# A merge pass of seven products on one Trainium2 core: the third and fourth product change places, one set of weights is loaded once instead of twice, and one sum moves to VectorE

## The chip, the cores and the metric

The kernel runs on one core of one Trainium2 chip. The metric is device time in microseconds (us) of one execution; the median of three runs is given. A profile of one further execution on the chip goes with it: a record of each instruction on TensorE (PE, with its weight loads as PEld), VectorE (DVE), ScalarE (ACT), GpSimd (POOL), and of each transfer issued by SyncE (SP).

## The reference

One step of a decoder layer, all in fp32: D = 1024, 2048 prompt tokens and 64 sample tokens, so 2112 in all. Two branches (sliding-window attention and gated linear attention) give `o_att` and `o_gla`; the tail below is where the change lies. `r_att` and `r_gla` are columns of the input projection of x.

```
z = einsum('btd,dn->btn', x, w_in)          # q, k, v, ..., r_att, r_gla
o_att, o_gla = attention branch, GLA branch
h      = o_att @ w_pa                       # K = 512
merged = sigmoid(r_att) * h + sigmoid(r_gla) * (o_gla @ w_pg)
y      = layer_norm(alpha * x + merged @ w_o)
```

The kernel's merge stage computes four products of the size (1024 x K) by (K x 2112): `w_pa` (K = 512), and `w_ra`, `w_rg`, `w_pg` (K = 1024 each).

## The kernel before

Products are in fp32 by two halves: an operand is split into a rounded part (`hi`, an ACT cast, L115) and the rest (`lo`, a DVE subtraction, L116), and each product is three matmuls, hi·hi, hi·lo and lo·hi (L1232 to L1234 in the merge stage). PE therefore waits for `wh`, `wl` of the weights and `xh`, `xl` of the tokens.

**The merge stage** lies from 1061.7 to 1644 us of the span. It goes through four passes, objects of the class `Pass`, one for each of the four weights, in the order `w_pa`, `w_ra`, `w_rg`, `w_pg`. Within a pass the matrix product is done as seven half-size products (Strassen's scheme in Winograd's form): weights and tokens are cut in two by two blocks, some products take sums of blocks, and the outputs are sums of products. `ORDER` sets the order of the seven. A product runs over MS = 3 token slices; such a (pass, product, slice) is a unit, and there are 4 x 7 x 3 = 84 of them, n = 0 to 83. A unit has NP4 = 4 column groups of 12 matmuls (6 in `w_pa`), each into one PSUM tile `pa` (five buffers) of 128 x 352.

**Weights.** `raw_w` loads a product's blocks into tiles `ws` (128 x 512 fp32, 256 KB; half of that in `w_pa`), four groups p = 0 to 3 each; `prep_w` forms the sums on POOL in place and splits into `wh`, `wl` (eight buffers each). Product 7 uses w11 − w21, product 6 uses s2 = w21 + w22 − w11, product 5 uses s1 = w21 + w22 and product 3 uses w12 − s2. Loads and splits for a product stand one product (three units) ahead of its use.

**Tokens.** `raw_x` loads `xs` (704 KB, three buffers; `xc` in `w_pa`), `prep_x` splits it into `xh`, `xl` (two buffers each), one unit ahead. The sums of token blocks that products 4 to 7 need are kept in DRAM (`ac_d`, `xc_d`, `uc_d`). Those for the fourth pass, `uc_d`, are formed within the third: at the start of each third unit, n = 42, 45, ... 57, `combine_load` loads two tiles `xc` (L857), `combine_do` forms four sums on POOL (L863 to L866) and stores them on SP (L868).

**Results.** `combine` adds `pa` into tiles `a12` and `a21` (12 buffers each) or a final `fin`. With product 1 in `a12`, product 7 is copied by ACT (L1078) into `a21`; product 6 is added to `a12` by DVE (L1081), and POOL then adds that to `a21` (L1082). The sinks at the end of each output store to `ha_d`, `tt_d` or `mg_d`; in the fourth pass `merge_sink` takes partners `cs` (L1064, four buffers, loaded on SP), a DVE operation (L1110), a POOL addition (L1111) and a store (L1113). The output projection and the normalization follow the merge stage.

Each engine, SP's issuing of transfers included, works its instructions in one fixed order, which a scheduler sets when the program is built, and which is not the order of the code. In it, the `wh` of a product can stand ahead of the `xh` of an earlier unit.

Of the kernel before, what the change touches and what calls it, by code (L numbers as in the profile page):

```python
# [16 lines left out]
ALU = mybir.AluOpType  # L17
# [4 lines left out]
P = 128  # L22
# [10 lines left out]
KT = D // P  # L33
# [18 lines left out]
def kernel(ctx, tc, io):  # L52
    nc = tc.nc
# [12 lines left out]
    def pd():  # L66
        return psd.tile([P, 512], F32, tag="pd", name="pd")

    def pa():
        return psa.tile([P, 512], F32, tag="pa", name="pa")  # L70
# [43 lines left out]
    def split(dst_h, dst_l, src, eng=nc.vector):  # L114
        pin["a"] = nc.scalar.copy(dst_h, src)  # L115
        i = eng.tensor_tensor(dst_l, src, dst_h.bitcast(F32), ALU.subtract)  # L116
        if eng is nc.vector:
            pin["d"] = i
# [3 lines left out]
    pin = {}  # L122
# [430 lines left out]
    for c, (t0, T) in enumerate(CHUNKS):  # L553
# [5 lines left out]
        A = {"kprev": kprev, "vprev": vprev, "q": [], "sil": []}  # L559
# [76 lines left out]
        ps = pd()  # L636
# [215 lines left out]
    def combine_load(new):  # L852
        src, dst, kh, k, s = combos.popleft()
        ts = slice(2 * s * MT, 2 * (s + 1) * MT)
        x1, x2 = new("x1")[:, :2 * MT], new("x2")[:, :2 * MT]
        for x_, k_ in ((x1, k), (x2, kh + k)):
            nc.sync.dma_start(x_, ug_d[k_ // 2][:, k_ % 2, ts] if src is None else src[:, k_, ts])  # L857
        return x1, x2, dst[:, :, s, k]

    def combine_do(x1, x2, dst, eng):  # L860

        t0, t1 = slice(0, MT), slice(MT, 2 * MT)
        eng.tensor_tensor(x2[:, t1], x2[:, t1], x1[:, t1], ALU.subtract)  # L863
        eng.tensor_tensor(x1[:, t1], x1[:, t1], x1[:, t0], ALU.subtract)
        eng.tensor_tensor(x1[:, t0], x1[:, t0], x2[:, t1], ALU.add)
        eng.tensor_tensor(x2[:, t0], x1[:, t0], x2[:, t0], ALU.subtract)  # L866
        for n_, x_ in ((0, x1), (2, x2)):
            nc.sync.dma_start(dst[n_:n_ + 2].rearrange("n p t -> p n t"), x_.rearrange("p (n t) -> p n t", n=2))  # L868
# [23 lines left out]
    for h in range(GH):  # L892
        W2 = {}
        wcap(16 + 6 * h)
        for c, (t0, T) in enumerate(CHUNKS):
# [15 lines left out]
            def combine():  # L911
                if sums:
                    with tc.issue_after(pin["d"].ins):
                        combine_do(*sums.pop(0), nc.vector)

            wv = [wt2("v", 0), wt2("v", 1)]
            for i in range((T + P - 1) // P):
                n = min(P, T - i * P)
                ps = pd()
# [20 lines left out]
            ps = pd()  # L940
            proj(ps[:, :T], wt2("k"), x, T)
            gla_k(B, ps[:, :T])
            combine()
            if len(CHUNKS) - 4 < c < len(CHUNKS) - 1:
                wload()
# [5 lines left out]
            ps = pd()  # L951
            proj(ps[:, :T], wt2("q"), x, T)
            gla_q(B, ps[:, :T])
            tick()
            combine()
            if end:
                chain(B)
            for m in range(2):
# [5 lines left out]
                ps = pd()  # L964
# [23 lines left out]
    ma = right.enter_context(tc.tile_pool(name="ma", bufs=1, side="right", reuse_waits="tile"))  # L988
    T = MT
    NP4 = 4  # L990
    ORDER = (1, 2, 7, 6, 5, 3, 4)
    FINAL = {2: (0, 0), 5: (1, 1), 3: (0, 1), 4: (1, 0)}

    def mtile(tag, n, bufs, dt=F32):
        pool = ma if tag in ("a12", "fin", "xc", "ws", "top") else mb
        return pool.tile([P, n], dt, tag=tag, name=tag, bufs=bufs)

    def toks(s, t):
        return slice((2 * s + t) * T, (2 * s + t + 1) * T)

    class Pass:
# [6 lines left out]

        def raw_w(self, i, p):
            out = []  # L1010
            for c, k in {1: [(1, 1)], 2: [(1, 2)], 7: [(1, 1), (2, 1)], 6: [(2, 1), (2, 2), (1, 1)], 5: [],
                         3: [(1, 2)], 4: [(2, 2)]}[i]:
                t = mtile("ws", KT // 2 * P, 11)[:, :self.kh * P]
                nc.sync.dma_start(t, self.w[c - 1, k - 1, p])
                out.append(t)
            return out

        def prep_w(self, i, p, r):
            A, tt = self.A, nc.gpsimd.tensor_tensor
            if i == 7:  # L1020
                tt(r[0], r[0], r[1], ALU.subtract)
            elif i == 6:
                tt(r[0], r[0], r[1], ALU.add)
                tt(r[2], r[0], r[2], ALU.subtract)
                A[p, "s1"], A[p, "s2"] = r[0], r[2]
            elif i == 3:
                tt(r[0], r[0], A.pop((p, "s2")), ALU.subtract)
            a = A[p, "s2"] if i == 6 else A.pop((p, "s1")) if i == 5 else r[0]
            hi, lo = (mtile(n, KT // 2 * P, 8, F32R)[:, :self.kh * P] for n in ("wh", "wl"))
            split(hi, lo, a)  # L1030
            return hi, lo
# [35 lines left out]
        def combine(self, i, p, s, ps, parts):  # L1067
            acc, z = self.acc, None
            add = nc.vector.tensor_tensor
            if i == 1:  # L1070
                a = acc[p, s, 12] = mtile("a12", T, 12)
                nc.scalar.copy(a, ps)
            elif i == 2:
                z = mtile("fin", T, 6)
                add(z, acc[p, s, 12], ps, ALU.add)
            elif i == 7:
                u = acc[p, s, 21] = mtile("a21", T, 12)
                nc.scalar.copy(u, ps)  # L1078
            elif i == 6:
                a, u = acc[p, s, 12], acc[p, s, 21]  # L1080
                add(a, a, ps, ALU.add)  # L1081
                pin["p"] = nc.gpsimd.tensor_tensor(u, u, a, ALU.add)  # L1082
            elif i == 5:
                a, z = acc[p, s, 12], mtile("fin", T, 6)
                add(z, acc[p, s, 21], ps, ALU.add)
                add(a, a, ps, ALU.add)
            elif i == 3:
                z = acc.pop((p, s, 12))
                add(z, z, ps, ALU.add)
            else:  # L1090
                z = acc.pop((p, s, 21))
                add(z, z, ps, ALU.subtract)
            if z is not None:
                c, t = FINAL[i]
                self.sink(z, parts, 2 * p + c, toks(s, t))
# [13 lines left out]
    def merge_sink(z, parts, ct, ts):  # L1109
# [8 lines left out]
              Pass(io["w_pg"], 4, None, uc_d, [tt_d], merge_sink)]  # L1118
    units = [(q, i, s) for q in passes for i in ORDER for s in range(MS)]
    groups = [(q, i, s, p) for q, i, s in units for p in range(NP4)]  # L1120

    plan = {n: [] for n in range(-2, len(units))}
    for n in range(0, len(units), MS):
        q, i, _ = units[n]
# [65 lines left out]

    for tag, n, bufs in (("a12", T, 12), ("fin", T, 6), ("xc", 2 * T, 5), ("ws", KT // 2 * P, 11), ("top", 640, 1),
                         ("xs", 4 * T, 3),
                         ("a21", T, 12), ("cs", 2 * T, 4), ("xh", KT // 2 * T, 2), ("xl", KT // 2 * T, 2),
                         ("wh", KT // 2 * P, 8), ("wl", KT // 2 * P, 8)):
        mtile(tag, n, bufs, F32R if tag[1] in "hl" else F32)
# [8 lines left out]
    for n, (q, i, s) in enumerate(units):  # L1206
        if n >= 2 * len(ORDER) * MS and n % 3 == 0 and combos:
            with tc.issue_after(pin["x"].ins), tc.issue_after(pin["p"].ins):
                combine_do(*combine_load(lambda t: mtile("xc", 2 * T, 5)), nc.gpsimd)
        if n >= 3 * len(ORDER) * MS and n % 4 == 0 and len(wo) < 4:  # L1210
            with tc.issue_after(pin["x"].ins), tc.issue_after(pin["a"].ins):
# [11 lines left out]
        for p in range(NP4):  # L1223
# [5 lines left out]
            ps = pa()[:, :T]  # L1229
# [209 lines left out]
```

## Time and profile before

| | |
|---|---|
| median of three runs | 1845.85 us (1841.35 to 1847.47) |
| the profiled execution's own time | 1846.22 us |
| its span | 1844.4 us |
| mean granted clock of PE | 0.992 of full speed |
| PE busy in the span | 98% |
| DVE, ACT, POOL busy | 69%, 46%, 23% |
| moved over the span | 315.84 MB, 171 GB/s |

All times below count from the start of the span. In the profile's rows an instruction is given with its line, engine, operation and tiles (out<-in), and behind it, in brackets, the idle time of its engine just before it and what ended that. SPq and ACTq rows are transfers issued by those engines, with the time that issuing took. In a row of stretches the columns are length, busy time of PE, PEld, DVE, ACT and POOL (each with the count of instructions), then the granted clock, the share of time in which the core's DMA engines were busy, and GB/s.

### The profile page before, as it was taken

What the parts mean: (1) busy time and instruction counts of PE and PEld (TensorE: products, weight loads), DVE (VectorE), ACT (ScalarE), POOL (GpSimd) and SP (SyncE); (2) the same over time, 40 slices, a digit from 0 to 9 for tenths busy, and PEclk for the clock granted to TensorE, in tenths of its full rate; (3) what the DMA queues carried; (4) which work ended last, traced back from release to release, by engine and by line L of the source; (5) the groups of instructions that cost most, each with busy time, mean ns of one, the idle gap of its engine ahead of it and who ended that gap; (6) DMA issues with size and microseconds to landing.
All of it is one profiled execution on the core that took longest, in us unless ns stands there. A gap on an engine that the chain in (4) does not pass through costs nothing.

```text
span 1844.4 us, 32399 instructions
## 1 busy us (share of the span) xinstructions
PE 1807.9 (98%) x11683; PEld 1722.2 (93%) x11683; DVE 1280.9 (69%) x2662; ACT 849.9 (46%) x1947; POOL 422.3 (23%) x559
## 2 busy tenths in 40 slices
PE   8999999999999999999999999999999999989997
PEld 7998988899999999999999999999999999988886
DVE  5677778767776776777667669648657566966655
ACT  5444545645665565656546453435443543211110
POOL 3310111300110111011110243430355153631111
PEclk9999999999999999999999999999999999999998
DMA  7211013534345444543543189858887967895531
GB/s 233 63 56 38 12 47 100 165 131 156 120 148 170 143 143 144 186 132 107 181 145 119 58 274 315 283 178 292 276 311 256 310 216 245 287 312 177 166 111 41
DMA packets 199554, 315.84 MB, mean 171 GB/s; under 512 B 21453, under 2 KB 161189, under 8 KB 199376
## 3 DMA queue, kind: packets, MB, share of 16 engines
q1 hardware_dynamic: 192624, 304.61, 50.5%
q0 software_dynamic: 5616, 7.58, 1.5%
q8 instruction: 92, 1.51, 0.3%
q10 hardware_dynamic: 1152, 1.57, 0.3%
q14 instruction: 70, 0.57, 0.1%
HBM read 228.52 MB, written 86.14 MB: 171 GB/s over the span
## 4 chain that ended last, share of the span: by engine, by line
PE 91%; DVE 3%; DMA 3%; issue 1%; POOL 1%; SPq 0%; ACT 0%; DVEq 0%; ACTq 0%; POOLq 0%
PE pd L185 11%; PE pd L187 11%; PE pd L186 11%; PE pa L1234 9%; PE pa L1233 9%; PE pa L1232 9%; PE pd L199 7%; PE pd L198 7%; PE pd L200 7%; PE pa L421 2%; DMA cs<-tt_d 1%; PE pa L406 1%; PE pa L755 1%; PE pa L753 1%; PE pa L754 1%
## 5 line engine op out<-in xcount | busy, mean ns | idle before, releaser
L185 PE MATMUL pd<-x,wh 128*128 128x384 f32 (+2 forms) x1248 | 409.1, 328 | 7.0 <-ACT x L115 6.3
L186 PE MATMUL pd<-x,wh 128*128 128x384 f32 (+2 forms) x1248 | 403.5, 323 | 0.6 <-DVE x L116 0.3
L187 PE MATMUL pd<-x,wl 128*128 128x384 f32 (+2 forms) x1248 | 403.1, 323 | 0.6 <-DVE wl L116 0.6
L1233 PE MATMUL pa<-xl,wh 128*128 128x352 f32 x1176 | 381.3, 324 | 7.9 <-DVE xl L116 7.6
L1232 PE MATMUL pa<-xh,wh 128*128 128x352 f32 x1176 | 381.4, 324 | 2.6 <-ACT xh L115 2.3
L1234 PE MATMUL pa<-xh,wl 128*128 128x352 f32 x1176 | 381.9, 325 | 0.0
L185 PEld LDWEIGHTS pd<-x,wh 128*128 128x128 f32 x1248 | 236.5, 190 | 17.2 <-issue 8.9
L186 PEld LDWEIGHTS pd<-x,wh 128*128 128x128 f32 x1248 | 236.5, 190 | 2.0 <-DVE x L116 1.5
L187 PEld LDWEIGHTS pd<-x,wl 128*128 128x128 f32 x1248 | 236.1, 189 | 1.0 <-DVE wl L116 1.0
L1233 PEld LDWEIGHTS pa<-xl,wh 128*128 128x128 f32 x1176 | 222.7, 189 | 10.4 <-DVE xl L116 10.1
L1232 PEld LDWEIGHTS pa<-xh,wh 128*128 128x128 f32 x1176 | 222.5, 189 | 3.6 <-ACT xh L115 2.6
L1234 PEld LDWEIGHTS pa<-xh,wl 128*128 128x128 f32 x1176 | 224.5, 191 | 0.0
L116 DVE TENSOR_TENSOR xl<-xs,xh 128x1408 fp32r<-128x1408 f32 x63 | 110.5, 1753 | 69.4 <-ACT xh L115 35.7
L198 PE MATMUL pd<-wh,x 128*128 128x256 f32 x512 | 147.9, 289 | 0.0
L199 PE MATMUL pd<-wh,x 128*128 128x256 f32 x512 | 145.6, 284 | 1.2 <-DVE x L116 1.1
L200 PE MATMUL pd<-wl,x 128*128 128x256 f32 x512 | 144.6, 282 | 0.0
L115 ACT CAST x<-xst 128x384 fp32r<-128x384 f32 (+2 forms) x164 | 78.2, 485 | 139.9 <-PE pd L199 117.9
L115 ACT CAST xh<-xs 128x1408 fp32r<-128x1408 f32 x63 | 86.5, 1372 | 103.9 <-PE pa L1234 81.7
L746 POOL TENSOR_SCALAR sq<-sq 128x1 f32<-128x1 f32 (+1 forms) x68 | 21.4, 314 | 467.2 <-ACT ring L745 467.2
L199 PE MATMUL pd<-woh,x 128*128 128x512 f32 x256 | 101.5, 396 | 0.0
L198 PE MATMUL pd<-woh,x 128*128 128x512 f32 x256 | 101.5, 396 | 0.0
L200 PE MATMUL pd<-wol,x 128*128 128x512 f32 x256 | 101.5, 396 | 0.0
(318 smaller groups left out, 3683.6 us busy)
## 6 DMA issues: line engine op xcount, KB each, us to landing
wst<-wt SPq DMA_DIRECT2D x33, 512.0 KB, 3.6
xs<-xc_d SPq DMA_DIRECT2D x24, 704.0 KB, 5.6
cs<-tt_d SPq DMA_DIRECT2D x48, 352.0 KB, 4.7
u<-xT SPq DMA_DIRECT2D x84, 192.0 KB, 4.0
xst<-xT SPq DMA_DIRECT2D x76, 192.0 KB, 2.6
xs<-xT SPq DMA_DIRECT2D x18, 704.0 KB, 5.9
ws<-w_ra SPq DMA_DIRECT2D x36, 256.0 KB, 4.4
ws<-w_rg SPq DMA_DIRECT2D x36, 256.0 KB, 5.6
```

The source lines that it names most:

```text
L115: pin["a"] = nc.scalar.copy(dst_h, src)
L116: i = eng.tensor_tensor(dst_l, src, dst_h.bitcast(F32), ALU.subtract)
L185: mm(ps, hi[:, s], xh[:, :T], start=(k == 0), stop=False)
L186: mm(ps, hi[:, s], xl[:, :T], start=False, stop=False)
L187: mm(ps, lo[:, s], xh[:, :T], start=False, stop=(k == n - 1))
L198: mm(ps, xh[:, xs], hi, start=(k == 0), stop=False)
L199: mm(ps, xl[:, xs], hi, start=False, stop=False)
L200: mm(ps, xh[:, xs], lo, start=False, stop=(k == KT - 1))
L421: mm(ot[pr, :], vb[:, pr], A["pT", bi, kv][:, hf], start=(hf == h0), stop=(hf == 1))
L1232: mm(ps, wh[:, ks], xh[:, ts], start=(k == 0), stop=False)
L1233: mm(ps, wh[:, ks], xl[:, ts], start=False, stop=False)
L1234: mm(ps, wl[:, ks], xh[:, ts], start=False, stop=(k == q.kh - 1))
```

## The change

Product 6 comes ahead of product 7. Product 6 loads three blocks for each group and forms three sums on POOL (lines L1023 to L1025 of the changed kernel): s1 = w22 + w21, s3 = w11 − w21, s2 = s1 − w11, each in place of a block. Product 7 then uses the kept s3 and loads nothing (before, it loaded two blocks and subtracted them); product 5 uses the kept s1 and product 3 the kept s2, as before. A pass has 28 loads of weights instead of 36. When product 7 is done, DVE adds `a12` (which has products 1 and 6 by then) and the PSUM tile into `a21` (L1082 of the changed kernel), in place of ACT's copy of product 7 and POOL's addition. `ws` has 12 buffers in place of 11, and the space comes from the filler `top`.

```diff
-    ORDER = (1, 2, 7, 6, 5, 3, 4)
+    WS, TOP = 12, 128
+    ORDER = (1, 2, 6, 7, 5, 3, 4)
...
-            for c, k in {1: [(1, 1)], 2: [(1, 2)], 7: [(1, 1), (2, 1)], 6: [(2, 1), (2, 2), (1, 1)], 5: [],
+            for c, k in {1: [(1, 1)], 2: [(1, 2)], 6: [(2, 2), (1, 1), (2, 1)], 7: [], 5: [],
                          3: [(1, 2)], 4: [(2, 2)]}[i]:
-                t = mtile("ws", KT // 2 * P, 11)[:, :self.kh * P]
+                t = mtile("ws", KT // 2 * P, WS)[:, :self.kh * P]
...
-            if i == 7:
-                tt(r[0], r[0], r[1], ALU.subtract)
-            elif i == 6:
-                tt(r[0], r[0], r[1], ALU.add)
-                tt(r[2], r[0], r[2], ALU.subtract)
-                A[p, "s1"], A[p, "s2"] = r[0], r[2]
+            if i == 6:
+
+                tt(r[0], r[0], r[2], ALU.add)
+                tt(r[2], r[1], r[2], ALU.subtract)
+                tt(r[1], r[0], r[1], ALU.subtract)
+                A[p, "s1"], A[p, "s2"], A[p, "s3"] = r
             elif i == 3:
                 tt(r[0], r[0], A.pop((p, "s2")), ALU.subtract)
-            a = A[p, "s2"] if i == 6 else A.pop((p, "s1")) if i == 5 else r[0]
+            a = A[p, "s2"] if i == 6 else A.pop((p, "s1" if i == 5 else "s3")) if i in (5, 7) else r[0]
...
+            elif i == 6:
+                a = acc[p, s, 12]
+                add(a, a, ps, ALU.add)
             elif i == 7:
                 u = acc[p, s, 21] = mtile("a21", T, 12)
-                nc.scalar.copy(u, ps)
-            elif i == 6:
-                a, u = acc[p, s, 12], acc[p, s, 21]
-                add(a, a, ps, ALU.add)
-                pin["p"] = nc.gpsimd.tensor_tensor(u, u, a, ALU.add)
+                pin["p"] = add(u, acc[p, s, 12], ps, ALU.add)
```

Most lines of the merge stage have in the changed kernel a number higher by one than before (L1014 has become L1015, L1027 L1028).

Over the program SP has 32 transfers fewer, ACT 48 instructions fewer, POOL 48 fewer and DVE 48 more; the order on PE is the same row by row. The order on the other engines moves. Three places follow; tiles carry their program's own numbers.

**POOL, third pass, units 43 to 46.** Here stand the sums for the third product's weights and the sums for `uc_d` of n = 42 and 45. Before, each of product 7's groups is one L1021:

```order
L1021 TENSOR_TENSOR ws_16722<-ws_16722,ws_16724 128x512
L863 TENSOR_TENSOR xc_16559<-xc_16559,xc_16558 128x352
L864 TENSOR_TENSOR xc_16558<-xc_16558 128x352
L865 TENSOR_TENSOR xc_16558<-xc_16558,xc_16559 128x352
L866 TENSOR_TENSOR xc_16559<-xc_16558,xc_16559 128x352
L1021 TENSOR_TENSOR ws_16806<-ws_16806,ws_16808 128x512
L863 TENSOR_TENSOR xc_16795<-xc_16795,xc_16794 128x352
L864 TENSOR_TENSOR xc_16794<-xc_16794 128x352
L865 TENSOR_TENSOR xc_16794<-xc_16794,xc_16795 128x352
L866 TENSOR_TENSOR xc_16795<-xc_16794,xc_16795 128x352
L1021 TENSOR_TENSOR ws_16894<-ws_16894,ws_16896 128x512
```

Now, on POOL as well, the sums of n = 45 and behind them product 6's groups p = 2 and p = 3:

```order
L863 TENSOR_TENSOR xc_16743<-xc_16743,xc_16742 128x352
L864 TENSOR_TENSOR xc_16742<-xc_16742 128x352
L865 TENSOR_TENSOR xc_16742<-xc_16742,xc_16743 128x352
L866 TENSOR_TENSOR xc_16743<-xc_16742,xc_16743 128x352
L1023 TENSOR_TENSOR ws_16754<-ws_16754,ws_16758 128x512
L1024 TENSOR_TENSOR ws_16758<-ws_16756,ws_16758 128x512
L1025 TENSOR_TENSOR ws_16756<-ws_16754,ws_16756 128x512
L1023 TENSOR_TENSOR ws_16848<-ws_16848,ws_16852 128x512
L1024 TENSOR_TENSOR ws_16852<-ws_16850,ws_16852 128x512
L1025 TENSOR_TENSOR ws_16850<-ws_16848,ws_16850 128x512
```

Behind the sums of n = 45 there stood one weight operation of the third product; now there are six, two groups of three.

**SP, the same place.** Before: the loads for the sums of n = 45, the last of product 7's blocks (ws_16894, ws_16896), and the first blocks of product 6:

```order
L857 DMA xc_16795<-ug3_d_75 128x704
L1014 DMA ws_16894<-w_rg 128x512
L1014 DMA ws_16896<-w_rg 128x512
L1014 DMA ws_16977<-w_rg 128x512
L1014 DMA ws_16979<-w_rg 128x512
L868 DMA uc_d_82<-xc_16794 128x2x352
L868 DMA uc_d_82<-xc_16795 128x2x352
L1045 DMA xs_16804<-xT 128x4x352
L1014 DMA ws_16981<-w_rg 128x512
```

Now, on SP, ws_16754 to 16758 are the blocks of product 6's group p = 2, and ws_16848 to 16852 those of p = 3:

```order
L857 DMA xc_16743<-ug3_d_75 128x704
L1015 DMA ws_16756<-w_rg 128x512
L1015 DMA ws_16758<-w_rg 128x512
L1015 DMA ws_16848<-w_rg 128x512
L1015 DMA ws_16850<-w_rg 128x512
L868 DMA uc_d_82<-xc_16742 128x2x352
L868 DMA uc_d_82<-xc_16743 128x2x352
L1046 DMA xs_16752<-xT 128x4x352
L1015 DMA ws_16852<-w_rg 128x512
```

All blocks of the third product stood ahead of the two stores of n = 45; now one of them, ws_16852, stands behind the stores and an `xs` load.

On ACT and DVE the casts and subtractions of these four weight groups stand in both kernels between the tokens of unit 45 and those of unit 46: `xh` of unit 45, four times a `wh` and a copy of product 1 (L1072, now L1073), `xh` of unit 46. The last two `wh` read ws_16806 and ws_16894 before, and read now ws_16756 and ws_16850, the outputs of L1025.

**POOL, fourth pass, from the third product on.** Before:

```order
L1023 TENSOR_TENSOR ws_18916<-ws_18916,ws_18918 128x512
L1024 TENSOR_TENSOR ws_18920<-ws_18916,ws_18920 128x512
L1027 TENSOR_TENSOR ws_19216<-ws_19216,ws_18739 128x512
L1027 TENSOR_TENSOR ws_19218<-ws_19218,ws_18745 128x512
L1111 TENSOR_TENSOR fin_18567<-fin_18567,cs_18480 128x352
L1027 TENSOR_TENSOR ws_19296<-ws_19296,ws_18836 128x512
L1111 TENSOR_TENSOR fin_18587<-fin_18587,cs_18497 128x352
```

Now:

```order
L1024 TENSOR_TENSOR ws_18564<-ws_18562,ws_18564 128x512
L1025 TENSOR_TENSOR ws_18562<-ws_18560,ws_18562 128x512
L1111 TENSOR_TENSOR fin_18493<-fin_18493,cs_18400 128x352
L1111 TENSOR_TENSOR fin_18513<-fin_18513,cs_18417 128x352
L1111 TENSOR_TENSOR fin_18533<-fin_18533,cs_18434 128x352
L1111 TENSOR_TENSOR fin_18553<-fin_18553,cs_18478 128x352
```

Product 6's sums stood among, and three of product 3's sums (L1027) ahead of, the first of product 2's L1111; now product 2's twelve L1111 follow the last weight sum one after the other, and product 3's sums stand behind them.

More of the change, by code (lines that the diff above doesn't have):

```diff
@@ L1189, in rest_m @@
         return [part(f, onew, samples=last) for f in load_m(t, u, n, last)]
-    for tag, n, bufs in (("a12", T, 12), ("fin", T, 6), ("xc", 2 * T, 5), ("ws", KT // 2 * P, 11), ("top", 640, 1),
+    for tag, n, bufs in (("a12", T, 12), ("fin", T, 6), ("xc", 2 * T, 5), ("ws", KT // 2 * P, WS), ("top", TOP, 1),
                          ("xs", 4 * T, 3),
```

## The prediction

> **What bounds the kernel now.** I read the busy shares and the chain first, then the merge stage by passes, then what TensorE waits for in it. The page's busy row, and the chain by engine:
>
> ```profile
> PE 1807.9 (98%) x11683; PEld 1722.2 (93%) x11683; DVE 1280.9 (69%) x2662; ACT 849.9 (46%) x1947; POOL 422.3 (23%) x559
> PE 91%; DVE 3%; DMA 3%; issue 1%; POOL 1%; SPq 0%; ACT 0%; DVEq 0%; ACTq 0%; POOLq 0%
> ```
>
> TensorE is the bound, and PE's order does not change. So the change can pay only where PE idles or runs at half clock, and cost only where it makes PE idle. The stretches of the four passes:
>
> ```profile
> 1061.70:1128.00 66.30, 63.82 (x374) 62.30 (x375) 49.05 (x91) 29.96 (x67) 30.77 (x31) 0.95 0.86 284
> 1128.00:1295.00 167.00, 166.89 (x1041) 166.30 (x1041) 122.35 (x190) 76.10 (x119) 40.16 (x30) 1.00 0.79 262
> 1295.00:1460.00 165.00, 165.00 (x1033) 165.00 (x1032) 104.03 (x134) 77.70 (x123) 70.53 (x56) 1.00 0.82 286
> 1460.00:1644.00 184.00, 176.40 (x1084) 175.10 (x1083) 132.54 (x180) 63.77 (x90) 89.73 (x69) 0.98 0.80 266
> ```
>
> Passes 2 and 3 (second and third rows) are full at clock 1.00; pass 4 idles 184.00 − 176.40 = 7.6 us, pass 1 2.5. The waits of PE from 1060 to 1650:
>
> ```profile
> PE pa L1233 <- DVE xl L116: 7.6, 5, 2.6
> PE pa L1232 <- ACT xh L115: 2.3, 1, 2.3
> ```
>
> Ten us, all for the tokens' halves: the entry, once in pass 1, twice in pass 4's product 7, twice in its last unit. No more can be won but the half clock that goes with them.
>
> **The change part by part.** What goes and comes, in groups of the merge stage:
>
> ```profile
> L1082 POOL TENSOR_TENSOR a<-a,a 128x352 f32<-128x352 f32 x48 | 55.6, 1176 | 52.1 <-DVE a L1081 51.9
> L1078 ACT COPY a<-pa 128x352 f32<-128x352 f32 x48 | 21.1, 455 | 22.4 <-PE pa L1234 22.4
> L1075 DVE TENSOR_TENSOR fin<-a,pa 128x352 f32<-128x352 f32 x48 | 24.3, 513 | 11.7 <-DMA tt_d<-fin 6.4 <-PE pa L1234 5.2
> L1021 POOL TENSOR_TENSOR ws<-ws 128x512 f32<-128x512 f32 (+1 forms) x16 | 21.0, 1318 | 127.0 <-ACT a L1101 49.3 <-DMA ha_d<-a 25.6 <-DMA ws<-w_pg 25.0
> ```
>
> Edits with one answer first. ACT loses 48 copies (21.1 us) at 46% busy: 0. POOL loses 48 sums (55.6 us); its weight sums stay 48 in number (16 L1021 become 16 L1025, 1.32 us each): 0 but for their places, below. DVE gains 48 adds out of PSUM of L1075's kind, 48 x 0.513 = 24.6 us, 2.05 in a unit of about 7.9 us (582 us for 63 units and 21 half ones): 0, as its 31% idle time covers it. In pass 1, where units are half as long, DVE is busy 49.05 of 66.30 us and gets 12 x 0.513 = 6.2; if that cover failed, the price is that of the gap which product 6's equal row of adds has there now, 0.9. SP loses 32 loads, 8 of 128 KB and 24 of 256 KB, 7.3 MB or 26 us at pass 1's 284 GB/s; with no wait of PE in passes 2 and 3 to shorten, 0 there. The 12th buffer: 0.
>
> *Pass 1, product 5.* POOL's run of sums, DVE's subtractions beside it, PE's wait from 1114 to 1118, and the group of pass 1's xl:
>
> ```profile
> 1106.33 12.72 POOL L1082 TENSOR_TENSOR a<-a,a 128x352 f32<-128x352 f32 x11
> 1111.28 1.22 DVE L116 TENSOR_TENSOR wl<-ws,wh 128x256 fp32r<-128x256 f32 x1
> 1115.04 0.74 DVE L116 TENSOR_TENSOR wl<-ws,wh 128x256 fp32r<-128x256 f32 x1
> 1115.70 1.63 DVE L116 TENSOR_TENSOR xl<-xc,xh 128x704 fp32r<-128x704 f32 x1
> PE pa L1233 <- DVE xl L116: 0.9, 1, 0.9
> L116 DVE TENSOR_TENSOR xl<-xc,xh 128x704 fp32r<-128x704 f32 x21 | 20.2, 960 | 4.7 <-ACT xh L115 4.6
> ```
>
> The xl that PE waits for took 1.63 beside POOL (the group's mean is 0.96), and the wl just before it were stretched too. With L1082 off POOL this goes: −0.9 (ends 0 and −0.9; the stretch, 0.67 on xl and 0.48 between the two wl, exceeds 0.9 together). [...]
>
> *Pass 3, the third product's weights.* This place has no wait of PE now, and the change makes one. POOL, SP, ACT and DVE there, and the landing time of a 256 KB block:
>
> ```profile
> 1327.04 0.95 POOL L863 TENSOR_TENSOR xc<-xc 128x352 f32<-128x352 f32 x1 [2.76 <-DMA xc<-ug_d]
> ...
> 1332.62 1.74 POOL L1021 TENSOR_TENSOR ws<-ws 128x512 f32<-128x512 f32 x1
> ...
> 1339.80 1.29 POOL L1024 TENSOR_TENSOR ws<-ws 128x512 f32<-128x512 f32 x1 [3.73 <-DMA ws<-w_rg]
> 1320.23 2.98 SPq L1014 DMA_DIRECT2D ws<-w_rg  x4
> 1331.33 1.73 SPq L868 DMA_DIRECT2D uc_d<-xc  x2
> 1333.12 0.46 SPq L1045 DMA_DIRECT2D xs<-xT  x1
> 1333.63 2.26 SPq L1014 DMA_DIRECT2D ws<-w_rg  x4
> 1334.39 0.62 ACT L115 CAST wh<-ws 128x512 fp32r<-128x512 f32 x1 [1.32 <-POOL ws L1021]
> 1335.26 1.38 ACT L115 CAST xh<-xs 128x1408 fp32r<-128x1408 f32 x1
> ...
> 1341.84 1.38 ACT L115 CAST xh<-xs 128x1408 fp32r<-128x1408 f32 x1 [0.91 <-PE pa L1234]
> 1336.97 1.61 DVE L116 TENSOR_TENSOR xl<-xs,xh 128x1408 fp32r<-128x1408 f32 x1
> ws<-w_ra SPq DMA_DIRECT2D x36, 256.0 KB, 4.4
> ```
>
> SP issues four blocks by 1323.2, then stands until POOL's sums of n = 45, late because their inputs land at 1327.04, release the stores at 1331.33; the xs and the next blocks go out behind them. POOL then has one L1021 (1332.62), ACT's fourth wh waits for it (1334.39), and xh of unit 46 follows at 1335.26. PE takes it up when unit 45 ends, at 1341.84, where xh of unit 47 finds its buffer freed. So ACT has about 3.5 us of slack.
>
> After the change POOL has six operations behind L866, not one, and the last block that group 3 needs, ws_16852, stands behind the two stores and an xs, where the block of L1024 stands now. Group 2: from 1332.62, three at 1.29 to 1.74: done 1336.5 to 1337.8. Group 3 waits for ws_16852, issued at about 1333.6 and landed by 1338.0 (4.4 us) to 1339.8 (when L1024 got its block); I take 1339.4, as the stores and the xs ahead of it are the same. Three sums at 1.29 and the steps between them, 4.0: 1342.0 to 1343.8. Then wh and copy (1335.26 − 1334.39 = 0.87), xh 1.38, xl 1.61: 3.9 more, 1345.9 to 1347.7, against 1341.84. One matmul of hi·hi can go ahead of xl, no more. PE idles 4.1 to 5.9 us; I take 5.4. ACT's copies and DVE's adds behind this wait free PSUM late, but by less than the tokens are late.
>
> What the clock does after such an idle is shown at the end of pass 4 (stretches 1574 to 1630 and 1632.5 to 1639.3, then DVE and ACT there):
>
> ```profile
> 1574.00:1630.00 56.00, 55.35 (x346) 54.92 (x344) 46.46 (x73) 10.63 (x10) 32.99 (x27) 1.00 0.96 317
> 1632.50:1639.30 6.80, 4.67 (x16) 4.67 (x17) 6.65 (x10) 3.57 (x9) 2.71 (x4) 0.50 0.98 311
> 1630.22 1.36 ACT L115 CAST xh<-xs 128x1408 fp32r<-128x1408 f32 x1 [10.37 <-DMA xst<-mg_d]
> 1631.57 0.53 DVE L1110 SCALAR_TENSOR_TENSOR a<-cs,a 128x352 f32<-128x352 f32 x1 [5.63 <-DMA cs<-tt_d]
> ```
>
> Two gaps of 2.3 and 2.6 us with one matmul between them are followed by 6.8 us at clock 0.50, in which PE worked 4.67 us: half of that, 2.3 us, is lost. The price of the clock in pass 3 is between 0 (as after the gaps of product 7, below) and 3.4 (all of 6.8); I take 2.4, since 5.4 us with one matmul inside is nearest to this row. Together +7.8 (4.1 to 9.3). [...]
>
> *Pass 4, products 2 and 7.* POOL, SP, DVE, and PE's waits from 1516 to 1532:
>
> ```profile
> 1497.44 1.30 POOL L1023 TENSOR_TENSOR ws<-ws 128x512 f32<-128x512 f32 x1 [12.88 <-DMA ws<-w_pg]
> 1507.83 5.62 POOL L1111 TENSOR_TENSOR fin<-fin,cs 128x352 f32<-128x352 f32 x4
> 1506.78 0.39 SPq L1064 DMA_DIRECT2D cs<-tt_d  x1
> 1517.71 0.53 DVE L1110 SCALAR_TENSOR_TENSOR fin<-cs,fin 128x352 f32<-128x352 f32 x1 [1.41 <-DMA cs<-tt_d]
> 1518.15 1.62 DVE L116 TENSOR_TENSOR xl<-xs,xh 128x1408 fp32r<-128x1408 f32 x1
> PE pa L1233 <- DVE xl L116: 2.8, 2, 1.6
> ```
>
> POOL stands 12.88 us for blocks, works weight sums until 1507.8, and its L1111 are late by that; the stores behind them and the cs loads behind those on SP start at 1506.78, DVE then waits for cs, and xl, behind that on DVE, is late twice: 2.8 us. Now no load belongs to product 7, its sums are done a product earlier, and the twelve L1111 follow each other. I take 85% of 2.8, −2.4 (ends 0 and −2.8).
>
> *The end of pass 4.* The three last products keep their loads, and the DMA engines are busy 96% from 1574 to 1630. The last xh came at 1630.22, its xs late behind cs loads and stores. DVE enters this part without L1082 beside it, which I estimate, from its stretched subtractions (as in pass 1's rows), to let the first results out 1.5 us sooner: −1.5 of the 4.9 idle (ends 0 and −4.9), and one chance in three that the half clock then does not come, −0.7 of 2.3.
>
> The sum: 1846.2 + 7.8 − 0.9 − 2.4 − 1.5 − 0.7 = 1848.5, against the profiled execution, which is 0.4 above the median of the runs: 1848.1.
>
> **The rivals.**
> *No stall in pass 3.* If SP's stores or ws_16852 came about 5 us earlier (inputs of n = 45 landing sooner, since fewer blocks go ahead of them), ACT's 3.5 us of slack would take up the rest. For it: 1319.08 to 1327 is a long landing. Against: the four blocks issued at 1320.23 are the same number in both orders, and POOL's six operations alone, with the load at no cost, end at 1332.6 + 7.9 = 1340.5, which with the 3.9 behind them is 1344.4, still 2.5 late. The time without the 7.8: 1840.3; if the end went altogether (4.9 and 2.3), 1836.
>
> *Slower: the stall stands and pass 4 gives nothing.* The place is SP in product 2 of pass 4: four cs buffers, each refilled behind a store that stands behind an L1111. If the refills stay late because the transfers themselves are slow there, and not POOL, xl stays late: DVE's 1.41 us waits at 1517.71, when POOL had long left its weight sums, speak for it; the DMA's idle time while POOL stood 12.88 us speaks against. Then 1848.1 + 2.4 + 1.5 + 0.7 = 1852.7. It decides once pass 4 gives less than 1.3 us, since slower begins at 1851.4.
>
> *Nothing to be seen.* All stalls hidden, or a stall of 2 to 3 us without the clock, weighed against the gains: 1843 to 1846.
>
> **How the numbers follow.** About 0.3% (5.5 us) is what a measurement of this kernel can tell from no change: 1840.3 to 1851.4. Forecast 0.55 (its own range 1845 to 1851.5, mostly same); no stall 0.20, of it 0.15 faster; slower rival 0.20; nothing to be seen 0.05. Faster 0.16, same 0.58, slower 0.26. For 8 in 10 the range goes from 1839.0, within the no-stall case, to 1853.5, past the slower one.
>
> **What would show it.** In the changed kernel's trace: a wait of PE for xl and xh near 1342 of 4 to 6 us, with clock 0.5 behind it and POOL's L1023 waiting for w_rg just before; no wait near 1116; none, or under 0.5, near 1518 and 1527; the end gap at 3 to 4 us. Wrong if pass 3 stays at clock 1.00 with PE full, if a new wait appears in passes 1, 2 or 4 where product 6's three blocks come a product earlier than product 7's two did, or if waits for cs on DVE in product 2 of pass 4 stay over 1 us.

## The result, and the profile after

The changed kernel takes 1854.03 us (median of five runs, 1850.36 to 1856.40), the kernel before 1845.85: a ratio of 1.0044, 95% interval 1.0024 to 1.0064. It is slower by 0.44%, above the predicted range's end of 1853.5. The profiled execution took 1856.40 us with a span of 1854.5, against 1846.22 and 1844.4. The ratios here and below leave out executions that took more than half as long again, and the one median that has such in it, that of the later sums, is 1843.8 without its two.

The page's busy row, and the stretches of the four passes of the merge stage (columns as before):

```profile
PE 1813.3 (98%) x11683; PEld 1726.4 (93%) x11683; DVE 1287.6 (69%) x2710; ACT 833.8 (45%) x1899; POOL 358.5 (19%) x511
...
1060.60:1128.00 67.40, 63.28 (x370) 60.80 (x371) 50.60 (x103) 26.75 (x55) 15.27 (x19) 0.97 0.91 306
1128.00:1295.00 167.00, 165.74 (x1035) 164.99 (x1034) 125.16 (x196) 70.52 (x104) 29.53 (x19) 1.00 0.74 240
1295.00:1460.00 165.00, 157.62 (x964) 156.96 (x963) 99.36 (x141) 67.89 (x104) 48.14 (x40) 0.97 0.76 254
1460.00:1654.00 194.00, 190.33 (x1163) 189.80 (x1163) 141.43 (x201) 66.31 (x88) 74.17 (x58) 0.98 0.79 260
```

The instructions moved as written: DVE 48 more, ACT and POOL 48 fewer. Pass 3, full before, has lost 7.4 us of PE and some clock; pass 4 has lost half of its idle; passes 1 and 2 have idle of a new kind. PE's waits from 1060 to 1660:

```profile
PE pa L1232 <- ACT xh L115: 8.5, 4, 6.4
PE pa L1233 <- DVE xl L116: 6.1, 6, 2.5
PE pa L1232 <- DVE a L1092: 1.1, 1, 1.1
PE pa L1232 <- ACT wh L115: 1.0, 2, 0.8
```

Since PE's order is the same in all kernels here, a unit's first matmul can be compared between traces. The table counts the matmuls of L1232 to L1234 (24 a unit in pass 1, 48 behind it) and gives how much longer a stretch of units took than in the kernel before, from the start of its first unit to the start of the unit named last (84 is the end); it holds idle and clock together. It is worked out from the traces, one execution each, so each column belongs to one execution. A second trace of the kernel before (last section) differs from the first by less than 0.2 us in every row but the last, where it is 1.5 shorter.

| units | where | changed | sums later | old loads | sum on POOL | other place | both |
|---|---|---|---|---|---|---|---|
| 0 to 3 | entry | +1.8 | +1.5 | +1.5 | +1.9 | −1.3 | −1.2 |
| 3 to 5 | pass 1, product 2 | +1.6 | +1.9 | +0.7 | +1.6 | −0.1 | −0.1 |
| 13 to 17 | pass 1, products 5, 3 | −2.6 | −2.6 | −2.3 | −0.6 | −2.7 | −2.7 |
| 19 to 22 | end of pass 1 | +1.9 | +1.6 | +3.0 | +2.2 | +2.0 | +1.4 |
| 45 to 47 | pass 3 | +10.4 | −0.1 | +7.1 | +8.9 | +10.5 | −0.1 |
| 68 to 71 | pass 4, third product (7 before, 6 now) | −3.2 | −3.5 | −3.2 | −3.2 | −3.2 | −3.5 |
| 82 to 84 | last units | −0.7 | −1.5 | −2.2 | −5.5 | −2.5 | −0.6 |

The columns behind the first are experiments, below. The changed kernel's column sums to +9.2; units 47 to 82 add 1.7 by a slower pace of PE (last section), and the merge stage began 1.1 earlier: with 0.3 of small rests that is the 10.1 us between the two spans. The table ends with the merge stage. Behind it the traces of its columns took as long as the kernel before, within 0.2 us, but for the old loads (2.3 longer), the sum on POOL (2.7) and the other place (4.9); why is not shown.

**The wait of pass 3.** The chain that ended last, in the changed kernel's trace (start, length, what):

```profile
1337.90 5.50 DMA ws<-w_rg
...
1343.57 1.27 POOL ws L1023
...
1344.91 1.27 POOL ws L1024
...
1346.25 1.27 POOL ws L1025
...
1348.51 1.27 ACT xh L115
...
1349.81 1.63 DVE xl L116
...
1351.49 0.66 PE pa L1233
```

It goes block, three sums, xh, xl, matmul, as the prediction had it. What held the block, on POOL and SP, then ACT, and the clock behind it:

```profile
1330.54 1.77 POOL L863 TENSOR_TENSOR xc<-xc 128x352 f32<-128x352 f32 x1 [15.66 <-DMA xc<-ug_d]
1322.40 0.85 SPq L857 DMA_DIRECT2D xc<-ug_d  x2
1335.03 2.31 SPq L868 DMA_DIRECT2D uc_d<-xc  x2
1337.39 0.46 SPq L1046 DMA_DIRECT2D xs<-xT  x1
1337.90 0.55 SPq L1015 DMA_DIRECT2D ws<-w_rg  x1
1340.04 0.62 ACT L115 CAST wh<-ws 128x512 fp32r<-128x512 f32 x1 [7.21 <-POOL ws L1025]
1347.54 0.62 ACT L115 CAST wh<-ws 128x512 fp32r<-128x512 f32 x1 [6.53 <-POOL ws L1025]
1346.20:1356.40 10.20, 5.57 (x18) 5.20 (x19) 6.09 (x8) 5.41 (x9) 1.26 (x1) 0.50 0.43 129
```

SP stood from 1326.7 to 1335.0 for the stores, as POOL's sums began only at 1330.54; the last block went out at 1337.90, 4.3 us later than the block of the same place before (1333.63), while PE had come only 1.7 later to unit 45. ACT waited twice, 13.7 us.

### The profile page after: what moved, and what is told of

The parts are those of the page before. It is cut to its first block, busy times and chain, and to the rows that moved or that the text cites. A ratio compares the mean times of both kernels' runs of the same rounds, so it can differ in the third digit from the quotient of the medians.

```text
span 1854.5 us, 32210 instructions
## 1 busy us (share of the span) xinstructions
PE 1813.3 (98%) x11683; PEld 1726.4 (93%) x11683; DVE 1287.6 (69%) x2710; ACT 833.8 (45%) x1899; POOL 358.5 (19%) x511
## 4 chain that ended last, share of the span: by engine, by line
PE 89%; DMA 3%; DVE 3%; ACT 2%; issue 1%; POOL 1%; SPq 0%; DVEq 0%; POOLq 0%; ACTq 0%
PE pd L185 10%; PE pd L186 10%; PE pd L187 10%; PE pa L1234 9%; PE pa L1233 8%; PE pa L1232 8%; PE pd L199 7%; PE pd L200 6%; PE pd L198 6%; PE pa L421 2%; PE pa L406 1%; PE pa L754 1%; PE pa L755 1%; PE pa L753 1%; PE pa L731 1%
## 5 line engine op out<-in xcount | busy, mean ns | idle before, releaser
L1232 PE MATMUL pa<-xh,wh 128*128 128x352 f32 x1176 | 383.1, 326 | 10.6 <-ACT xh L115 8.5
L1233 PE MATMUL pa<-xl,wh 128*128 128x352 f32 x1176 | 381.5, 324 | 6.1 <-DVE xl L116 6.1
L1234 PE MATMUL pa<-xh,wl 128*128 128x352 f32 x1176 | 383.4, 326 | 0.0
L1232 PEld LDWEIGHTS pa<-xh,wh 128*128 128x128 f32 x1176 | 222.6, 189 | 12.9 <-ACT xh L115 9.6
L1233 PEld LDWEIGHTS pa<-xl,wh 128*128 128x128 f32 x1176 | 224.5, 191 | 7.9 <-DVE xl L116 7.9
L1234 PEld LDWEIGHTS pa<-xh,wl 128*128 128x128 f32 x1176 | 223.8, 190 | 0.5 <-DVE wl L116 0.3
L116 DVE TENSOR_TENSOR xl<-xs,xh 128x1408 fp32r<-128x1408 f32 x63 | 106.3, 1688 | 58.9 <-ACT xh L115 42.7
```

Of the source, the lines that this page charges most:

```text
L1232: mm(ps, wh[:, ks], xh[:, ts], start=(k == 0), stop=False)
L1233: mm(ps, wh[:, ks], xl[:, ts], start=False, stop=False)
L1234: mm(ps, wl[:, ks], xh[:, ts], start=False, stop=(k == q.kh - 1))
```

## The experiments

The comparison is always with runs of the kernel before on the same chip. Times and ratios come from several executions, the table's entries from one trace; with a spread of 0.2 to 0.3% from execution to execution, the traces carry most verdicts on single terms.

**Sums for uc_d later.** The changed kernel with

```diff
-        if n >= 2 * len(ORDER) * MS and n % 3 == 0 and combos:
+        if n >= 2 * len(ORDER) * MS + 2 * MS and n % 2 == 0 and combos:
```

> The changed kernel, with the six sums for uc_d begun at units 48, 50, ... 58 instead of 42, 45, ... 57, when no blocks of product 6 are under way. Collision theory (the idle of pass 3 comes from product 6's six last weight sums and its last block standing behind the sums of n = 45 and their stores): PE full from unit 45 to 47, no half clock in pass 3; the 10.4 us between the starts of units 45 and 47 go, and with them the slower pace behind them if that hangs on the half clock: about 1842 to 1845. Rival, too many blocks (twelve blocks in the place of eight are late there whatever stands beside them): a wait of PE of 4 us or more remains at unit 46: 1850 or more. Rival, DVE's 48 adds: no change, 1854.

Measured 1844.34 us, ratio 0.9996 (0.9979 to 1.0012). There is no wait of PE between 1320 and 1360 and no half clock in pass 3; the other rows of the table move by less than 0.9 us. The wait belongs to product 6's weights meeting the sums of n = 45, not to the twelve blocks by themselves, nor to DVE's adds.

**The stores on another queue.** In `combine_do`:

```diff
-            nc.sync.dma_start(dst[n_:n_ + 2]...)
+            (nc.gpsimd if eng is nc.gpsimd else nc.sync).dma_start(dst[n_:n_ + 2]...)
```

> The changed kernel with the stores of the sums for uc_d issued by POOL's own queue, so that SP does not stand for POOL. In the order, all blocks of product 6 then go out without waiting for the sums, and the weight sums of group 2 stand ahead of the sums of n = 45; those of group 3 stay behind them. Collision theory by SP (the late last block is the larger part): the wait of pass 3 falls from 8 us to 3 or less, 1845 to 1849. Collision theory by POOL (the six sums behind the sums of n = 45 are the larger part): 4 us or more remain, 1850 to 1853.

Measured 1847.57 us, ratio 1.0016 (1.0004 to 1.0027). Units 45 to 47 lose 1.1 us in place of 10.4. On POOL, ACT and PE there (POOL's L1024 to L1026 and PE's L1234 are the lines L1023 to L1025 and L1233 of the other kernels):

```profile
1336.71 1.31 POOL L1024 TENSOR_TENSOR ws<-ws 128x512 f32<-128x512 f32 x1
1340.79 0.62 ACT L115 CAST wh<-ws 128x512 fp32r<-128x512 f32 x1 [5.83 <-POOL ws L1026]
PE pa L1234 <- DVE xl L116: 0.9, 1, 0.9
```

The last group's sums still stand behind those of n = 45, and ACT still waits 5.83 us, but they need no block any more (no idle in front of L1024), and PE waits 0.9. Two things moved here at once, the block out from behind SP's stores and the second group's sums ahead of those of n = 45; together they are nearly all of the wait. Three sums behind those of n = 45 are covered but for 0.9. This trace lost 7.9 us behind the merge stage, with a half clock of 6.8 us there, and that is in its time; why is not shown.

**Old loads.** New order, DVE's sum and 12 buffers, with product 6's two sums and product 7's own two blocks as before:

```diff
-            for c, k in {..., 6: [(2, 2), (1, 1), (2, 1)], 7: [], ...
+            for c, k in {..., 6: [(2, 1), (2, 2), (1, 1)], 7: [(1, 1), (2, 1)], ...
...
+            if i == 7:
+                tt(r[0], r[0], r[1], ALU.subtract)
+            elif i == 6:
+                tt(r[0], r[0], r[1], ALU.add)
+                tt(r[2], r[0], r[2], ALU.subtract)
+                A[p, "s1"], A[p, "s2"] = r[0], r[2]
```

> The changed kernel with the old weights: product 6 forms s1 and s2 (two sums for a group), product 7 loads its two blocks and subtracts them; the new order, DVE's sum and the 12 buffers stay. Collision theory: product 6 stands at the sums of n = 45 as in the changed kernel, with four sums behind them instead of six: the wait of PE at unit 46 comes, 2 to 3 us shorter than 7.9 us; 1850 to 1853. Rival, the kept s3 (one loading of weights) is what costs: no wait there, 1846 to 1848. Rival, DVE's adds: 1854.

Measured 1851.32 us, ratio 1.0028 (1.0013 to 1.0042), as the collision theory has it: 7.1 us in units 45 to 47, 3.3 less than with three sums a group. So keeping s3 is not most of what costs; product 6's three blocks standing third is. The other 3.3 went with the third sum of each group. Outside the table's rows this trace loses 2.0 us in units 5 to 13 and waits 1.5 for PSUM near unit 49.

**The old sum.**

```diff
-                pin["p"] = add(u, acc[p, s, 12], ps, ALU.add)
+                nc.scalar.copy(u, ps)
+                pin["p"] = nc.gpsimd.tensor_tensor(u, u, acc[p, s, 12], ALU.add)
```

> The changed kernel with the old sum: ACT copies product 7 out of PSUM and POOL adds a12 to it; the new order and the one loading stay. Collision theory: the wait of pass 3 stays within 1 us of 7.9; the units 13 to 17 of pass 1 get slow again by about 2.6 us as POOL's sums come back beside DVE: 1856 to 1858. Rival, DVE's 48 adds cost the time: 1848 or less.

Measured 1855.02 us, ratio 1.0044 (1.0027 to 1.0061). DVE's 48 adds cost nothing that shows; they save 2.0 of the 2.6 us in units 13 to 17. The gain at pass 4's third product stays at 3.2 without them, and with the old loads too: neither makes it, and the order is what is left. (The next run, in the old order, gains 2.0 there as well, behind a loss at the start of the pass.) The time came out 1 us under the expectation. PE waited 5.8 us in pass 3 in place of 7.4, more of a change than expected: it came to unit 45 3.8 us later than in the changed kernel, and the last block went out only 2.1 later (1339.96). The last units gained 5.5 us, with no half clock there; why is not shown.

**Layout alone.** The kernel before with 12 buffers:

```diff
-    ("ws", KT // 2 * P, 11), ("top", 640, 1),
+    ("ws", KT // 2 * P, 12), ("top", 128, 1),
```

> The kernel before, with 12 buffers ws and a filler of 128, all else as before. Layout theory (the loss at the entry and in product 6 of pass 1 comes from the twelfth buffer, which takes memory that the stage ahead still uses, so that SP's second load of weights waits about 8 us and all behind it): SP's second load is issued near 1062 instead of 1054, unit 3 starts 1.5 to 2 us later against unit 0 than before, 1847.5 to 1849. Rival, more blocks (the twelve blocks of product 6 alone make that loss): SP issues as before, the units of pass 1 start as before, 1846.

Measured 1853.44 us, ratio 1.0047 (1.0028 to 1.0065), more than expected. SP's issuing of the first four loads of weights (start, time for the four), in the kernel before, the changed one and this one:

```profile
1053.17 1.90 SPq L1014 DMA_DIRECT2D ws<-w_pa  x4
```

```profile
1052.08 10.25 SPq L1015 DMA_DIRECT2D ws<-w_pa  x4
```

```profile
1049.67 10.27 SPq L1014 DMA_DIRECT2D ws<-w_pa  x4
```

The second of the four waits about 8 us, and all loads behind it: the layout theory's sign, in the old order as well. What it waits for is DVE's work on `S`, the state of the GLA branch, in the stage ahead; in the changed kernel SP's waits have it as

```profile
SPq L1015 <- DVE S L840: 8.1, 1, 8.1
```

and the kernel before has no such wait. Units 0 to 3 lose 1.1 us, units 3 to 5 nothing. But the larger loss of this kernel is elsewhere, 5.3 us in units 63 to 65 at the start of pass 4, where the changed kernel has none. There ACT stands for a load of the output projection's weights, `w_o`, ahead of the `wh` and `xh` that PE waits for; in the kernel before, in this one, and in the control further below:

```profile
1471.00 1.05 ACT L115 CAST woh<-wst 128x1024 fp32r<-128x1024 f32 x1 [1.76 <-DMA wst<-w_o]
```

```profile
1478.35 1.05 ACT L115 CAST woh<-wst 128x1024 fp32r<-128x1024 f32 x1 [6.51 <-DMA wst<-w_o]
```

```profile
1470.62 1.05 ACT L115 CAST woh<-wst 128x1024 fp32r<-128x1024 f32 x1 [5.99 <-DMA wst<-w_o]
```

SP issued that load at 1464.73 before and at 1472.41 here. So this run shows the wait at the entry, but its time does not price it.

**Another place.** The changed kernel with its buffers in another order in memory:

```diff
-    for tag, n, bufs in (("a12", T, 12), ("fin", T, 6), ("xc", 2 * T, 5), ("ws", ..., WS), ("top", TOP, 1),
+    for tag, n, bufs in (("fin", T, 6), ("xc", 2 * T, 5), ("ws", ..., WS), ("top", TOP, 1), ("a12", T, 12),
```

> The changed kernel with its 12 buffers at another place in memory: fin, xc, ws, filler, a12 in this order instead of a12, fin, xc, ws, filler, so that no load of the first product waits for VectorE and ScalarE. Layout theory (the second load of weights, which stands 8 us on SP, is what delays the entry and product 6's blocks in pass 1): unit 3 stands against unit 0 as in the kernel before, where the changed kernel is 1.8 us later, and product 6's blocks reach POOL near 1073, so that the 1.5 us of units 3 to 5 shrink too; the wait in pass 3 stays near 8 us: 1850 to 1853. Rival, the twelve blocks alone: units 0 to 5 as in the changed kernel, 1854.

Measured 1849.21 us, ratio 1.0038 (1.0023 to 1.0052). SP and POOL in this kernel, and POOL in the changed one:

```profile
1052.12 1.87 SPq L1015 DMA_DIRECT2D ws<-w_pa  x4
1069.96 0.88 POOL L1023 TENSOR_TENSOR ws<-ws 128x256 f32<-128x256 f32 x1 [7.10 <-DMA ws<-w_pa]
```

```profile
1075.97 1.45 POOL L1023 TENSOR_TENSOR ws<-ws 128x256 f32<-128x256 f32 x1 [13.14 <-DMA ws<-w_pa]
```

SP does not stand, product 6's sums begin 6 us earlier, and units 0 to 5 lose 4.7 us less, with the same twelve blocks. So the layout, not the number of blocks, made the loss at the entry. The one in units 3 to 5 takes both, since the layout alone did not have it in the old order. The wait of pass 3 is as large as in the changed kernel.

**Both.** The other place and the later sums.

> The changed kernel with both: the other place in memory and the sums for uc_d begun at units 48, 50, ... 58. If the losses of pass 3 (10.4 us) and of the entry (1.8, and 1.5 in product 6) are each what the two theories say and add up, this is the sum of both gains: 1839 to 1842, faster than the kernel before. If the entry's loss comes from the twelve blocks: as with the later sums alone, 1844.

Measured 1836.87 us, ratio 0.9962 (0.9945 to 0.9979). It beats both kernels, by more than was expected; about 3 us of that is PE's pace in the traced execution (last section). Once more:

> The fastest version once more (other place in memory, later sums for uc_d), for its time and its pace. Its first trace had TensorE at 158.9 ns a matmul in the merge stage, the fastest of three levels. If the level belongs to the execution, another level may show here, and the median over all executions lies at 1836 to 1840, 0.2 to 0.5% under the kernel before; if it belongs to the kernel, 158.9 again and 1837.

Measured 1838.37 us, ratio 0.9966 (0.9951 to 0.9980). The change is thus worth about 0.35% to the kernel before, once its two side effects are taken out. Not all of that need be the change's own: units 0 to 3 take 0.9 to 1.2 us less than in the kernel before, and the other place was not tried in the old order.

**Control: later sums in the kernel before.** The first edit, in the old order.

> The kernel before with the sums for uc_d begun at units 48, 50, ... 58. Collision theory: the sums cost the kernel before nothing at their old place, since ACT has 3.5 us of slack there, so moving them gains nothing: 1845 to 1847, unless they now meet the sums of product 3 (slower). Rival (the sums' place costs both kernels, and moving them is a gain of its own): 1842 or less.

Measured 1847.35 us, ratio 1.0017 (1.0004 to 1.0030): no gain, rather a loss of 2 to 3 us. In the trace 2.6 us are lost in units 63 to 65, at ACT's wait for `w_o` shown above. The place of the sums cost the old order nothing, and the gain above is no general one.

**The end of pass 1.** In the changed kernel POOL and DVE, near unit 19:

```profile
1138.09 1.30 POOL L1023 TENSOR_TENSOR ws<-ws 128x512 f32<-128x512 f32 x1 [33.73 <-DMA ha_d<-a]
1138.54 1.40 DVE L116 TENSOR_TENSOR wl<-ws,wh 128x512 fp32r<-128x512 f32 x1
1139.86 1.98 DVE L116 TENSOR_TENSOR xl<-xc,xh 128x704 fp32r<-128x704 f32 x1
1141.77 1.78 DVE L116 TENSOR_TENSOR wl<-ws,wh 128x512 fp32r<-128x512 f32 x1
```

Behind these stand the L1092 that free PSUM, for which PE waits 1.1 us. Two runs tested whether POOL's sums beside them are the cause. The first forms s3 when product 7 is prepared, on top of both edits:

```diff
-                tt(r[0], r[0], r[2], ALU.add)
-                tt(r[2], r[1], r[2], ALU.subtract)
-                tt(r[1], r[0], r[1], ALU.subtract)
-                A[p, "s1"], A[p, "s2"], A[p, "s3"] = r
+                tt(r[2], r[0], r[2], ALU.add)
+                tt(r[1], r[2], r[1], ALU.subtract)
+                A[p, "s3"], A[p, "s2"], A[p, "s1"] = r
+            elif i == 7:
+                tt(A[p, "s3"], A[p, "s3"], A[p, "s2"], ALU.subtract)
```

> Both edits of the fastest version (the other place in memory, the sums for uc_d later) and s3 formed when product 7 is prepared, as w22 - s2, so that product 6 has two sums a group on POOL, as in the kernel before, and product 7 one. Contention theory for the end of pass 1 (units 19 to 22, 1.4 to 2.0 us lost in every kernel with product 6 third, because POOL's sums for pass 2 stand beside VectorE's subtractions there): a third of POOL's sums goes from there, the loss falls to about 1 us or less; 1835 to 1838. Rival (the loss comes from the loads' time or the order of products, not from the number of sums): 1.4 to 2.0 as before; 1836 to 1838. By time alone the two can't be told apart, by the units' starts they can.

Measured 1841.79 us, ratio 0.9992 (0.9980 to 1.0004), above the expectation, and units 19 to 22 lose 1.5 as before: the number of sums is not it. The second holds product 6's loads of pass 2 back:

```diff
-        nc.sync.dma_start(ha_d[:, ct, ts], z)
+        pin["s"] = nc.sync.dma_start(ha_d[:, ct, ts], z)
...
+            if i == 6 and q is passes[1]:
+                with tc.issue_after(pin["s"].ins):
+                    raws[u, p] = q.raw_w(i, p)
```

> The fastest version (other place in memory, later sums for uc_d) with the loads of product 6's blocks of pass 2 held back on SP behind the last store of pass 1, so that POOL forms their sums after pass 1 and not beside VectorE's subtractions at its end. The sums' number made no difference there (1.39 with three a group, 1.50 with two). Contention theory: units 19 to 22 lose 0.5 us or less against the kernel before, VectorE's subtractions there take 0.7 to 0.9 us again, PE has no wait for L1092. Rival (the loss at the end of pass 1 comes from the loads of pass 2's tokens or from the pass's own end): 1.4 us as before. If the blocks then come too late for product 6 of pass 2, a wait of PE near 1190 shows it. The time alone: 1835 to 1837 or 1837.

Measured 1840.48 us, ratio 0.9991 (0.9977 to 1.0004). The same DVE instructions, and POOL's first sum of pass 2:

```profile
1134.02 0.69 DVE L116 TENSOR_TENSOR wl<-ws,wh 128x512 fp32r<-128x512 f32 x1
1134.76 0.89 DVE L116 TENSOR_TENSOR xl<-xc,xh 128x704 fp32r<-128x704 f32 x1
1135.57 0.68 DVE L116 TENSOR_TENSOR wl<-ws,wh 128x512 fp32r<-128x512 f32 x1
1156.63 1.28 POOL L1023 TENSOR_TENSOR ws<-ws 128x512 f32<-128x512 f32 x1 [56.58 <-DMA ws<-w_ra]
```

Together 2.26 us instead of 5.16, and units 19 to 22 lose 0.0: shown to be POOL's sums, run early, beside DVE's subtractions. The loads, which this run moved too, are not the cause: over the merge stage of the changed kernel the 67 subtractions of 128x512 with no POOL sum beside them took 0.68 to 0.69 us each, and the 17 beside one 0.68 to 1.78. DVE's adds out of PSUM show no such stretch: in the kernel before the 31 of the 48 L1075 that stood beside a POOL sum took 505 to 522 ns, the other 17 took 504 to 522. As a version it came out above the 1837 us expected and gains nothing, since the blocks then come late in pass 2: PE waits 1.5 and 1.2 us there, and units 22 to 45 lose 3.8 us with a half clock of 3.4.

## Why the prediction was wrong

The forecast was 1848.1 us, the measured median 1854.0. The table sets the prediction's terms against the units of the changed kernel's trace; they are not a difference of medians.

| term | predicted | trace |
|---|---|---|
| pass 3 | +7.8 | +10.4 |
| 12th buffer | 0 | +3.4 (entry 1.8, product 6's blocks in pass 1 1.6) |
| POOL's weight sums, same in number | 0 | +1.9 (end of pass 1) |
| pass 1, product 5 | −0.9 | −2.6 |
| pass 4, product 7 | −2.4 | −3.2 |
| end of pass 4 | −2.2 | −0.7 |
| pace of PE | none | +1.7 (last section) |

*The step that failed* is "The 12th buffer: 0". I priced it as a buffer and not as a place in memory. With it a `ws` of the first product lies where the stage ahead still had its state `S`; SP's second load now stood 8.1 us for that, and the place run shows 4.7 us between the two layouts (the 3.4 of the table, and 1.3 by which the other place is better than the kernel before). The prediction's working starts at the third product and leaves out the entry, where the new wait stands. It named a new wait in pass 1 as a sign of being wrong, and gave it no price.

*The second* is "0 but for their places": I checked the new places in pass 3 and pass 4 and not the end of pass 1, where three sums of pass 2 now run beside DVE; held back, the loss was 0.0.

*Pass 3* was right in mechanism and place (SP's stores, the last block behind an xs, ACT's wh ahead of xh, xl last) and too small in size. I took the sums of n = 45 to run when they ran before. They began at 1330.54 in place of 1327.04, with PE only 1.7 us later. And the half clock lasted 10.2 us where I had taken the 6.8 of the end's row: PE worked 5.57 us in it, at 293 ns a matmul where one took 161 behind it, so nearly half of that is lost. Of the 10.4 us, 7.4 are waits (predicted 5.4) and 3.0 the clock (2.4). The half clock began at 1346.2, 2.7 us into the wait of 6.4, and in the run that held product 6's loads back one of 3.4 us stood behind waits of 1.5 and 1.2. Inside the merge stage the half clocks lasted 6.8 and 6.8 us in the kernel before, and 3.4, 10.2 and 6.8 in the changed kernel; what sets the start and the length is not shown.

*The gains* were two too small and one too large. Pass 1's was counted only as the one wait of 0.9, but the units behind it were slow too (18.05 us for four that took 15.4 after the change), as DVE came into products 5 and 3 with a backlog; with the sum back on POOL 2.0 of it returns. The gain of pass 4's third product came also where product 7 kept its loads, so the loads that I gave as one reason were not needed. The end of pass 4 kept most of its idle, though I had a part of it go. Why is not shown. Two traces of the kernel before differ by 1.5 us there, so the −0.7 says little; and with the sum on POOL the last units took 5.5 us less, without a half clock, so the end is not set by transfers alone that the change leaves as they were.

*The rivals.* The first, no stall in pass 3, is what the later sums made true, by an edit and not by earlier landing. The second had the sign but not the mechanism: product 7's waits went, as predicted. The third, nothing to be seen, did not come. No rival had the layout. Two figures of the working were a little off: without the whole end the first rival's sum is 1835.3, not 1836, and the view of the waits has 0.3 us for a `wh` beside those for the tokens' halves.

## What to carry to other kernels

A larger pool moves everything allocated with it, so look at which loads have new waits on the stage ahead before calling a buffer free; a filler may have been holding that place for a reason. When work is put earlier in a fixed order, look for what stands in its new neighbourhood on each queue: here a store that waits for POOL held back loads on SP (the last block went out 4.3 us later), and sums run early slowed VectorE (three subtractions took 5.16 us in place of 2.26). A saving of 7 MB and of 48 POOL operations was worth about 0.35%, but only after a layout and an order had been put right.

## What the runs showed of the hardware

In the merge stage of these traces TensorE's steady pace stood at one of three levels. In the stretch from 1380 to 1460, busy all the time at clock 1.00, the kernel before, the changed kernel, the fastest version and the same version once more show these counts of matmuls (first number in brackets):

```profile
1380.00:1460.00 80.00, 80.00 (x502) 80.00 (x501) 52.09 (x77) 35.73 (x53) 30.18 (x26) 1.00 0.80 275
```

```profile
1380.00:1460.00 80.00, 80.00 (x499) 80.00 (x498) 50.95 (x79) 32.25 (x46) 16.33 (x15) 1.00 0.75 246
```

```profile
1380.00:1460.00 80.00, 80.00 (x505) 80.00 (x504) 52.62 (x77) 36.09 (x55) 26.33 (x18) 1.00 0.83 288
```

```profile
1380.00:1460.00 80.00, 80.00 (x502) 80.00 (x501) 51.65 (x78) 34.60 (x53) 28.44 (x20) 1.00 0.81 282
```

By the starts of matmuls that is 160.0, 161.1, 158.9 and 160.0 ns each. Most changes of level came at a wait or a half clock, though not every one, which the expectation below has: in the changed kernel near 1130 the level went from 161.1 to 158.9 ns with neither. The fastest version had two levels in two executions, and a further profile of the kernel before tells the same:

> The kernel before itself, for its trace. TensorE's steady pace had three levels in the traces so far, 158.9, 160.0 and 161.1 ns a matmul, changing only at a half clock or a long wait. If the level belongs to the execution and not to the kernel, this trace may show another level than the 160.0 ns of the first, and its time goes by 3.4 us for a level over the merge stage; if it belongs to the kernel, 160.0 ns again and 1846.

Measured 1844.76 us, ratio 1.0006 (0.9989 to 1.0022). It kept 160.0 ns up to pass 4, and went to 161.1 after the waits of product 7 there; from 1540 to 1620, this execution, then the first one:

```profile
1540.00:1620.00 80.00, 80.00 (x499) 80.00 (x498) 64.22 (x96) 22.37 (x26) 43.24 (x37) 1.00 0.79 257
```

```profile
1540.00:1620.00 80.00, 80.00 (x502) 80.00 (x501) 65.24 (x96) 24.02 (x28) 43.49 (x36) 1.00 0.79 261
```

So the level belongs, at least there, to the execution and not to the kernel. One level is 1.1 ns a matmul, 53 ns a unit, 3.4 us over passes 2 to 4: of the size of the spread between executions (eight of the run just above took 1842.9 to 1847.9 us). What sets it stays open. The changed kernel's 161.1 began behind the half clock of pass 3, so the 1.7 us of its slower pace may be the execution's or that half clock's; the runs do not tell which.
